# Operand buffers of the matrix products placed at a fixed distance modulo 256 bytes

## The chip, the core and the metric

The kernel runs on one core of a Trainium2 chip, as one program in one launch. The metric is the time of one execution in device microseconds (us); smaller is better. In the kernel before, the median of three runs is 2753.42 us (2751.35 to 2754.86).

A core has a tensor engine (PE in the profile) that multiplies a stationary operand (up to 128 x 128, loaded first, "PEld") with a moving operand (128 rows and up to 512 columns that stream through), both from the on-chip memory SBUF, into the accumulators PSUM; a vector engine (DVE), a scalar engine (ACT), a general one (POOL), and queues that start DMA transfers (SP above all). SBUF has 128 partitions; an address here is a byte offset inside a partition, the same for all 128.

## The reference

256 tokens of width 1024, batch 1, float32. A first block of two layers and a second of four layers follow one another:

```
for layer in range(2):
    x = x + 0.5 * swiglu(rmsnorm(x), ffn1_w_in, ffn1_w_out)      # 1024 -> 2 x 2816 -> 1024
    h = rmsnorm(x)
    x = x + (attn_lru_mixer(h) if layer == 0 else deltanet_mixer(h))
    x = x + cross_attention(rmsnorm(x), rmsnorm(mem))            # mem: 256 x 1024
    x = x + 0.5 * swiglu(rmsnorm(x), ffn2_w_in, ffn2_w_out)
x = rmsnorm(x)
for i, mixer in enumerate((retention, conformer_conv, gla, retention)):
    x = x + rmsnorm(mixer(rmsnorm(x)))
    x = x + rmsnorm(relu(rmsnorm(x) @ w_up) ** 2 @ w_down)       # 1024 -> 4096 -> 1024
```

Nearly all of the arithmetic is in products of the 256 tokens with float32 weight matrices.

## The kernel before, in words

**Values in two parts.** Activations are kept transposed, channels on partitions, tokens along the free dimension, so a chunk of 128 channels is a tile of 128 x 256. For accuracy each operand of a product with weights is split into a high part and a rest, both of type float32r, and three products are made: high weights with both parts of the activations, the weights' rest with the high part (`mm3`, line 204; `mm_split`, line 252, does the same for attention values). All go through `mm` (line 201), so in the profile nearly all products have line 202.

**Weights.** The weight matrices come from memory as one long stream of pieces, each of 8 blocks of 128 x 128 (512 KB), in the order of use. `fetch` (line 158) loads a piece into one of three `raw` buffers (SP queue). `block` (line 166) splits it: ACT copies it to `whi` (line 179), DVE subtracts to get `wlo` (line 180); five buffers of each (pool `wp`). A block serves three products of 256 columns, so a piece serves 24.

**Products.** `gemm` (line 211) has the weight block stationary and the activations moving, 256 columns; either the inputs are the outer loop (all outputs' high-part products first, then those with the activations' rest) or it takes one output after the other with `mm3`. `gemm_rows` (line 236) makes outputs with tokens on partitions: there the activations are stationary and four weight blocks move, 512 columns. Outputs take turns in four PSUM banks (pool `ps`).

**Moving operands by name.** `xs`: the normalised input of a layer, split (pool `xsp`, four buffers, `prep` at line 353). `h`: the hidden values of the feed-forward parts (`ffn`, line 528, and `mlp`, line 1703), input of their second matrix. `os`: what a mixer or an attention hands to its output matrix. `memS`: the memory's normalised values in cross-attention (`xa`, line 555). `kq`: the delta-net's output (`dn`, line 792). `pr`, `mem`, `pT`, `pts`: attention weights, multiplied with the values `v`.

**Order and memory.** Engines run their instructions in the order of the program; waits are semaphores that the tile layer sets by data dependence. Each layer opens a pool of its own (`stage`, line 131) and gets tiles from it with `T` (a tag with its number of buffers, line 139) and `one` (line 142); pools that last all along (`cp`, `rawp`, `wp`, `xsp` and others) lie below in SBUF, one after the other in the order of creation. No tile asks for an alignment; a tile starts where the one before ends, and pools are padded.

```
def T(self, tag, shape=(2, S), dt=F32, bufs=2, p=128):
    return self.pool.tile([p, *shape], dt, name=self.nm(tag), tag=tag, bufs=bufs)
```

Of the kernel before, what the change touches and what calls it, by code (L numbers as in the profile page):

```python
# [7 lines left out]
F32 = mybir.dt.float32  # L8
F32R = mybir.dt.float32r
# [8 lines left out]
S = 256  # L18
# [14 lines left out]
CONV_STEP = (3, 6)  # L33

# [27 lines left out]
class Lazy:  # L62
    """A norm's factors, emitted in two steps: the sums, then (when first asked for) the values."""
# [16 lines left out]
class Kernel:  # L80
    def __init__(self, ctx, tc, A):
        self.ctx, self.tc, self.nc, self.A = ctx, tc, tc.nc, A
        nc = self.nc

        def pool(name, bufs, **kw):
            return ctx.enter_context(tc.tile_pool(name=name, bufs=bufs, **kw))

        self.cp = pool("cp", 1)
        self.rawp = pool("rawp", 3)
        self.wp = pool("wp", 5)  # L90
        self.xsp = pool("xsp", 4)
        self.tp = pool("tp", 2)
        self.sp = pool("sp", 4)
        self.psp = pool("ps", 4, space=bass.MemoryType.PSUM)
        self.pmp = pool("pm", 4, space=bass.MemoryType.PSUM)
        self.order = []
        self.piece = -1
        self.at = NB
        self.x, self.ready, self.next_gain, self.hold = [], [], None, {}
        self.n, self.raws = 0, []  # L100
        self.par = self.cp.tile([128, N_PAR], F32, name="par")
        nc.scalar.dma_start(self.par[:, 0:16], A["par"][:, 0:16])
        for p in range(4):
            t = self.cp.tile([128, 2, S], F32, name=f"x{p}")
            nc.sync.dma_start(t, A["x"][:, 2 * p:2 * p + 2, :])
            self.x.append(t)
            if p < 2:
                self.fetch(p, 2 - p)
        nc.scalar.dma_start(self.par[:, 16:], A["par"][:, 16:])
        self.ident = self.cp.tile([128, 128], F32, name="ident")  # L110
        nc.scalar.dma_start(self.ident, A["ident"])
        self.ones = self.cp.tile([128, 128], F32, name="ones")
        nc.gpsimd.memset(self.ones, 1.0)
        self.inv = self.cp.tile([128, 2], F32, name="inv")
        nc.gpsimd.memset(self.inv[:, 0:1], 1.0 / D)
        nc.gpsimd.memset(self.inv[:, 1:2], 1.0 / 512)
        self.onesw = self.cp.tile([128, S], F32, name="onesw")
        nc.gpsimd.memset(self.onesw, 1.0)
        self.both = self.cp.tile([128, 8], F32, name="both")
        nc.vector.tensor_tensor(self.both, self.P("final_norm", 0, 8), self.P("norm_gains_2", 0, 8), op=OP.mult)  # L120
# [9 lines left out]
    @contextmanager  # L130
    def stage(self):
        """The memory of one part of the computation."""
        with ExitStack() as es:
            old = getattr(self, "pool", None)
            self.pool = es.enter_context(self.tc.tile_pool(name=self.nm("st"), bufs=1))
            yield
            self.pool = old

    def T(self, tag, shape=(2, S), dt=F32, bufs=2, p=128):
        return self.pool.tile([p, *shape], dt, name=self.nm(tag), tag=tag, bufs=bufs)  # L140
# [17 lines left out]
    def fetch(self, piece, n=1):  # L158
        """Loads a piece of the weights, in n transfers."""
        raw = self.rawp.tile([128, NB * 128], F32, name=self.nm("raw"), tag="raw")  # L160
        w = NB * 128 // n
        for i in range(n):
            self.nc.sync.dma_start(raw[:, i * w:i * w + w], self.A["w"][piece][:, i * w:i * w + w])
        self.raws.append(raw)
# [26 lines left out]
    def hold_back(self, ahead, act, dve):  # L191
        """The split of the pieces so many ahead comes after these instructions."""
        for n in ahead:
            self.hold.setdefault(self.piece + n, []).append((act, dve))

    def behind(self, ins, other):
        """Queues ins behind other on their engine."""
        if other is not None:
            self.tc.add_manual_dep(ins.ins, other.ins.name, mybir.DependencyInfo(mybir.DependencyClass.NoSync, mybir.DependencyReason.DATA), reason="behind")
# [11 lines left out]
    def gemm(self, name, groups, src, k_outer, calls={}):  # L211
        """groups: psum pairs with the m of each half; k_outer walks the inputs in the outer loop.
        calls: what to emit after step n (an input or, without k_outer, an output)."""
# [22 lines left out]
    def gemm_rows(self, name, m0, src, calls={}):  # L236
        """Outputs [token, 512 columns]: two banks, one for each 128 tokens."""
        outs = [self.psum((512,)) for _ in range(2)]
        nk = len(src)
        for k in range(nk):  # L240
            wh, wl = self.block(name, k, m0, 4)
            xh, xl = src[k]
            for t, o in enumerate(outs):
                s = slice(t * 128, t * 128 + 128)
                self.mm(o, xh[:, s], wh, k == 0, False)
                self.mm(o, xh[:, s], wl, False, False)
                self.mm(o, xl[:, s], wh, False, k == nk - 1)
            if k in calls:
                calls[k]()
        return outs  # L250

    def mm_split(self, out, a, b, first, last):
        """out (+)= a.T @ b, both given as (hi, lo)."""
# [4 lines left out]
    def split_rows(self, v, outs, y):  # L258
        """v [128, 2 (hi, lo), 2, 512] from two psum tiles scaled by token."""
# [4 lines left out]
    def split(self, t, src_ap, scale=1.0):  # L264
        """t [128, 2 (hi, lo), 2, 256] from a pair."""
# [8 lines left out]
    def rsqrt(self, ms, w, tag="rs"):  # L274
        """1/sqrt of a [128, w] tile."""
# [16 lines left out]
    def quick_rsqrt(self, ms):  # L292
        """-2/sqrt of each column of a [128, 2] psum, the columns in turn."""
# [20 lines left out]
    def token_sums(self, tiles, one=None):  # L314
        """Sums over partitions of [128, 256] tiles: a [128, 2] psum with tokens on partitions."""
# [9 lines left out]
    def rows(self, cols, pb=None):  # L325
        """Per-token values [128, 2] as a psum [128, 256] with the value of token t in column t."""
# [5 lines left out]
    def add_square(self, acc, sq, p, eps=EPS):  # L332
        """Adds pair p of squares up; after the last one, both halves too."""
# [10 lines left out]
    def stats(self, acc, one=None):  # L344
        """-2/sqrt of the sums over partitions of acc times one; one's inverse times EPS / 128 is in acc."""
# [7 lines left out]
    def prep(self, src, x, gain, tiles=None):  # L353
        """Appends the split parts of pair x times its gains to src."""
        nc = self.nc
        t = self.xsp.tile([128, 2, 2, S], F32R, name=self.nm("xs"), tag="xs") if tiles is None else tiles()
# [7 lines left out]
    def updated(self, p):  # L364
        """Pair p of x is final in this part: its split for the next part."""
# [3 lines left out]
    def norm(self, x, gain, tiles=None, rbt=None):  # L369
        """x: four pairs. Returns the split inputs times the gain, and (to be called) each token's factor as columns and as rows."""  # L370
# [19 lines left out]
    def two_norms(self):  # L390
        """As norm, for rmsnorm(rmsnorm(x) * final_norm): the factors of both norms together, and the first one's rows."""
# [48 lines left out]
    def residual(self, name, src, scale, first=1):  # L440
        """x += scale * (src @ w); the first pairs of outputs walk the inputs together."""
# [16 lines left out]
    def post_norm(self, name, src, gain, bias=None):  # L458
        """x += rmsnorm(src @ w [+ bias]) * gain."""
# [61 lines left out]
    def keep_clock(self, t, n):  # L521
        """Products nobody reads, for the time in which the tensor engine would wait and lose its clock."""
# [32 lines left out]
    def xa(self, l):  # L555
        nc = self.nc
        with self.stage():
# [62 lines left out]
            for n in range(2):  # L620
                outs = self.gemm_rows(("xa_wkv", l), 8 + 4 * n, msrc, {1: rest[0], 3: rest[1], 7: rest[2]} if n == 0 else {})
                v = self.T("v", (2, 2, 512), F32R, 1)
# [11 lines left out]
    def gate_half(self, name, c, w):  # L634
        """Half of a parameter, as a small tile."""
# [4 lines left out]
    def log1p_exp(self, z, w):  # L640
        """log(1 + exp(-|z|)) of a [128, w] tile, by the series of atanh."""
# [25 lines left out]
    def softplus_neg(self, z, w):  # L667
        """softplus(-z) = max(-z, 0) + log(1 + exp(-|z|))."""
# [123 lines left out]
    def dn(self):  # L792
        nc = self.nc
        W = ("dn_w_in", 0)
        with self.stage():
# [18 lines left out]
            wab = self.one((8, 16))  # L814
# [14 lines left out]
            def parts(m, after):  # L829
                """The product's quarters; after the last one, what becomes of it."""  # L830
# [12 lines left out]
            def conv_silu(m, out, g):  # L843
                """out [128, 2, 256]: twice the silu of the convolution."""
# [13 lines left out]
            def gates():  # L858
                """beta / 4, log of beta's inverse, the sums of the log decays."""
# [56 lines left out]
            def decays(b):  # L916
                """Exponents of four heads: rows and, per source, columns."""
# [94 lines left out]
            def level_2(lev, p):  # L1012
                """The even columns of the inverse and the odd ones of its transpose."""
# [103 lines left out]
            def weave(main, side):  # L1117
                """Emits both lists, the second spread over the first."""
# [89 lines left out]
    def rotary_tables(self):  # L1208
        """cos and sin of position * frequency, frequencies on partitions: reduced by multiples of 2 pi in three parts."""
# [31 lines left out]
    def ret(self, i, final=False):  # L1241
# [3 lines left out]
        with self.stage():  # L1245
# [72 lines left out]
            for h in range(4):  # L1318
# [14 lines left out]
                vs[h] = self.T("v", (2, 2, 512), F32R, 1)  # L1333
# [22 lines left out]
    def conv(self, i):  # L1356
# [3 lines left out]
        with self.stage():  # L1360
# [75 lines left out]
            def about_six():  # L1436
                """Sums over six chunks of the distance to their mean and of its square."""
# [94 lines left out]
    def gla(self, i):  # L1532
        nc = self.nc
        W = ("gla_w_in_2", 0)
        with self.stage():
            w1 = self.one((8, 64))
# [7 lines left out]
            wmr = self.one((128,))  # L1544
# [65 lines left out]
            def values(n, calls={}):  # L1610
                outs = self.gemm_rows(W, 8 + 4 * n, src, calls)
                v = self.one((2, 2, 512), F32R)
# [3 lines left out]
            def scores(h):  # L1616
                q, k = qk[0][:, h], qk[1][:, h]
                ptile = self.T("ptl")
                for d in range(2):
# [9 lines left out]
                    # (source tile, queries, columns of the query tile)  # L1629
# [99 lines left out]
def stages(k):  # L1729
    """Each part of the computation with the gains of its first norm."""  # L1730
# [30 lines left out]
def chunks(v):  # L1761
    """[..., 128 c] to [128, ... c] with the vector's place in the first axis."""
# [90 lines left out]
```

## Time and profile before

| | |
|---|---|
| median of three runs | 2753.42 us (2751.35 to 2754.86) |
| span of the profiled execution (first to last instruction) | 2748.4 us |
| mean granted clock of the tensor engine | 0.994 |
| PE busy | 2708.3 us, 99% of the span, 21804 products |
| DVE busy | 1892.7 us, 69% |
| ACT busy | 1419.8 us, 52% |
| POOL busy | 81.6 us, 3% |
| DMA | 449.17 MB, mean 163 GB/s |

The profile gives the profiled execution's time as this span alone; the runs' median lies 5.0 us above it. A row of the costliest groups reads: line, engine, operation, output tile <- input tiles, shapes, count | busy us, mean ns of one. For a product the first input named is the moving operand. A product's duration counts from its start to its modelled end; products overlap, so their durations sum to more than the time. A row of a timeline reads: start us, us from the first start to the last end, engine, line, operation, and how many equal instructions in a row it merges. A row of the windows reads: stretch in us, its length, then busy us and (x count) of PE, PEld, DVE, ACT and POOL, then the granted clock, the DMA engines' busy share and GB/s. A wait reads: who <- for whom: us in total, times, longest us.

### The profile page before, as it was taken

What the parts mean: (1) busy time and instruction counts of PE and PEld (TensorE: products, weight loads), DVE (VectorE), ACT (ScalarE), POOL (GpSimd) and SP (SyncE); (2) the same over time, 40 slices, a digit from 0 to 9 for tenths busy, and PEclk for the clock granted to TensorE, in tenths of its full rate; (3) what the DMA queues carried; (4) which work ended last, traced back from release to release, by engine and by line L of the source; (5) the groups of instructions that cost most, each with busy time, mean ns of one, the idle gap of its engine ahead of it and who ended that gap; (6) DMA issues with size and microseconds to landing.
All of it is one profiled execution on the core that took longest, in us unless ns stands there. A gap on an engine that the chain in (4) does not pass through costs nothing.

```text
span 2748.4 us, 52619 instructions
## 1 busy us (share of the span) xinstructions
PE 2708.3 (99%) x21804; PEld 2639.8 (96%) x21804; DVE 1892.7 (69%) x3043; ACT 1419.8 (52%) x2005; POOL 81.6 (3%) x102
## 2 busy tenths in 40 slices
PE   8999999999999999999999999989999999999998
PEld 8998999999999999999999999989999999899998
DVE  7757867657678676766876756877468764876754
ACT  5446554444457655545455544346447654545553
POOL 0000000000010000000000001800000000000000
PEclk9999999999999999999999999989999999999999
DMA  6554545555543144555544654225544555445553
GB/s 221 184 194 134 189 153 178 185 182 185 184 157 127 63 154 158 183 184 177 165 159 155 199 187 150 85 74 195 185 153 142 160 184 189 155 146 185 169 184 123
DMA packets 125343, 449.17 MB, mean 163 GB/s; under 512 B 14192, under 2 KB 15216, under 8 KB 125104
## 3 DMA queue, kind: packets, MB, share of 16 engines
q1 hardware_dynamic: 121680, 440.46, 49.4%
q10 hardware_dynamic: 3424, 5.37, 0.6%
q8 instruction: 170, 2.79, 0.4%
q14 instruction: 69, 0.57, 0.1%
HBM read 444.72 MB, written 1.05 MB: 162 GB/s over the span
## 4 chain that ended last, share of the span: by engine, by line
PE 93%; DVE 3%; ACT 1%; DMA 1%; POOL 1%; issue 1%; SPq 0%; POOLq 0%; DVEq 0%; ACTq 0%
PE ps L202 84%; PE pm L202 9%; DVE wlo L180 1%; DMA raw<-w 1%; POOL pacc L1398 0%; ACT whi L179 0%; POOL dg L1475 0%; DVE pt L512 0%; DVE x L513 0%; DVE xs L360 0%; DVE pt L506 0%; DMA one<-gla_w 0%; PE pm L767 0%; PE pm L581 0%; ACT XX L1025 0%
## 5 line engine op out<-in xcount | busy, mean ns | idle before, releaser
L180 DVE TENSOR_TENSOR wlo<-raw,whi 128x1024 fp32r<-128x1024 f32 (+1 forms) x837 | 1025.6, 1228 | 553.1 <-ACT whi L179 551.8
L179 ACT ACTIVATE whi<-raw 128x1024 fp32r<-128x1024 f32 (+1 forms) x837 | 884.0, 1058 | 987.8 <-PE ps L202 778.6
L202 PE MATMUL ps<-xs,whi 128*128 128x256 f32 x7424 | 1360.8, 285 | 7.3 <-ACT whi L179 6.8
L202 PEld LDWEIGHTS ps<-xs,whi 128*128 128x128 f32 x7424 | 1163.8, 192 | 11.5 <-ACT whi L179 6.8
L202 PE MATMUL ps<-xs,wlo 128*128 128x256 f32 x3712 | 1039.9, 284 | 0.3 <-DVE wlo L180 0.3
L202 PEld LDWEIGHTS ps<-xs,wlo 128*128 128x128 f32 x3712 | 713.8, 192 | 2.2 <-issue 1.3
L202 PE MATMUL ps<-h,whi 128*128 128x256 f32 x3456 | 610.9, 279 | 0.0
L202 PEld LDWEIGHTS ps<-h,whi 128*128 128x128 f32 x3456 | 527.7, 187 | 0.0
L202 PE MATMUL ps<-h,wlo 128*128 128x256 f32 x1728 | 473.0, 279 | 0.0
L202 PEld LDWEIGHTS ps<-h,wlo 128*128 128x128 f32 x1728 | 324.6, 188 | 0.0
L202 PE MATMUL ps<-os,whi 128*128 128x256 f32 x1152 | 205.5, 281 | 3.4 <-ACT os L267 3.4
L202 PEld LDWEIGHTS ps<-os,whi 128*128 128x128 f32 x1152 | 177.8, 190 | 4.2 <-ACT os L267 3.7
L202 PE MATMUL ps<-os,wlo 128*128 128x256 f32 x576 | 156.1, 281 | 0.0
L202 PE MATMUL ps<-whi,xs 128*128 128x512 f32 x352 | 113.9, 397 | 0.0
L437 DVE TENSOR_TENSOR t<-ps,rbc 128x512 f32<-128x512 f32 x116 | 79.6, 690 | 48.2 <-PE ps L202 45.6
L202 PEld LDWEIGHTS ps<-os,wlo 128*128 128x128 f32 x576 | 109.6, 190 | 0.0
L202 PEld LDWEIGHTS ps<-whi,xs 128*128 128x128 f32 x352 | 65.9, 188 | 13.2
L267 ACT ACTIVATE h<-t 128x512 fp32r<-128x512 f32 x108 | 67.9, 629 | 18.1 <-DVE t L550 16.5
L269 DVE TENSOR_TENSOR h<-t,h 128x512 fp32r<-128x512 f32 x108 | 74.3, 688 | 0.8 <-ACT h L267 0.5
L359 ACT ACTIVATE xs<-x,par 128x256 fp32r<-128x256 f32 x120 | 53.9, 499 | 32.2 <-DVE x L508 20.9
L202 PE MATMUL ps<-wlo,xs 128*128 128x512 f32 x176 | 69.1, 393 | 0.7 <-DVE wlo L180 0.6
L1717 DVE SCALAR_TENSOR_TENSOR t<-ps,rbc 128x512 f32<-128x512 f32 x64 | 43.8, 690 | 30.3 <-PE ps L202 29.7
(425 smaller groups left out, 2425.0 us busy)
## 6 DMA issues: line engine op xcount, KB each, us to landing
raw<-w SPq DMA_DIRECT2D x835, 512.0 KB, 3.6
mem<-mem ACTq DMA_DIRECT2D x8, 256.0 KB, 5.2
x<-x SPq DMA_DIRECT2D x4, 256.0 KB, 5.8
os<-ret_dist ACTq DMA_DIRECT2D x2, 512.0 KB, 3.8
out<-x SPq DMA_DIRECT2D x4, 256.0 KB, 2.3
raw<-w SPq DMA_DIRECT2D x2, 256.0 KB, 4.8
one<-lru_w ACTq DMA_DIRECT2D x1, 512.0 KB, 4.6
par<-par ACTq DMA_DIRECT2D x1, 333.5 KB, 4.9
```

The lines of the kernel that those rows point to most:

```text
L179: a = nc.scalar.activation(hi[:, i:i + w], raw[:, i:i + w], AF.Copy)
L180: b = nc.vector.tensor_tensor(lo[:, i:i + w], raw[:, i:i + w], hi[:, i:i + w].bitcast(F32), op=OP.subtract)
L202: self.nc.tensor.matmul(out, lhsT, rhs, start=start, stop=stop, skip_group_check=True)
L267: nc.scalar.activation(t[:, 0], src_ap, AF.Copy, scale=scale)
L269: nc.vector.tensor_tensor(t[:, 1], src_ap, t[:, 0].bitcast(F32), op=OP.subtract)
L359: nc.scalar.activation(t[:, 0, i], x[:, i], AF.Copy, scale=g)
L437: self.nc.vector.tensor_tensor(t, ps, self.bc(rb), op=OP.mult)
L1717: nc.vector.scalar_tensor_tensor(a, g[0], 0.0, self.bc(rb), op0=OP.max, op1=OP.mult)
```

## The change

Buffers move; the computation stays. A filler of 48 float32 (`cpad`, 192 bytes) is put into the pool `cp`, so that all that lies behind it starts 192 bytes later, the weight buffers among them. The tiles of the moving operands named in `MOVING`, and `xs`, are aligned to 256 bytes. The tiles of attention values are made 64 bytes longer and used from byte 64 on (`values_tile`). Three small tiles of the delta-net and the gated layer are put into buffers of other tags (`c2`, `ptl`), which takes no room of their own. The docstrings and one comment are dropped.

```diff
+MOVING = ("h", "os", "memS", "kq", "pr", "pts", "mem", "pT")
...
         nc.gpsimd.memset(self.inv[:, 1:2], 1.0 / 512)
+        self.cp.tile([128, 48], F32, name="cpad")
         self.onesw = self.cp.tile([128, S], F32, name="onesw")
...
     def T(self, tag, shape=(2, S), dt=F32, bufs=2, p=128):
-        return self.pool.tile([p, *shape], dt, name=self.nm(tag), tag=tag, bufs=bufs)
+        return self.pool.tile([p, *shape], dt, name=self.nm(tag), tag=tag, bufs=bufs, align_bytes=256 if tag in MOVING else None)
+
+    def values_tile(self, tag, bufs=1):
+
+        n = self.nm("v")
+        t = self.pool.tile([128, 2064], F32R, name=n, tag=tag or n, bufs=bufs, align_bytes=256)
+        return t[:, 16:].rearrange("p (a b c) -> p a b c", a=2, b=2)
...
-        t = self.xsp.tile([128, 2, 2, S], F32R, name=self.nm("xs"), tag="xs") if tiles is None else tiles()
+        t = self.xsp.tile([128, 2, 2, S], F32R, name=self.nm("xs"), tag="xs", align_bytes=256) if tiles is None else tiles()
...
-                v = self.T("v", (2, 2, 512), F32R, 1)
+                v = self.values_tile("v")
...
-            wab = self.one((8, 16))
+            wab = self.T("c2", (8, 16))
...
-                vs[h] = self.T("v", (2, 2, 512), F32R, 1)
+                vs[h] = self.values_tile("v")
...
-            w1 = self.one((8, 64))
+            w1 = self.T("ptl", (8, 64))
...
-            wmr = self.one((128,))
+            wmr = self.T("ptl", (128,))
...
-                v = self.one((2, 2, 512), F32R)
+                v = self.values_tile(None)
```

The two built programs have the same instructions in the same order on every engine, and the same waits but for one: ACT waits for DVE once more ahead of a `c2` tile of the delta-net layer. What differs is addresses. The profile shows no addresses; the table has them from the two programs. The distance is the start of the moving operand less that of the stationary one, in bytes, modulo 512 (modulo 256 in brackets). Within a kind it is the same for every product, since blocks and halves of tiles lie multiples of 512 bytes apart.

| moving, stationary (products of float32r) | columns | products | distance before | distance after |
|---|---|---|---|---|
| xs, weights | 256 | 11136 | 0 (0) | 192 (192) |
| h, weights | 256 | 5184 | 320 (64) | 192 (192) |
| os, weights: two retention layers, gated layer | 256 | 768 + 192 | 320 (64) | 192 (192) |
| os, weights: two cross-attention layers | 256 | 384 | 320 (64) | 448 (192) |
| os, weights: first mixer | 256 | 192 | 448 (192) | 192 (192) |
| os, weights: convolution layer | 256 | 192 | 0 (0) | 448 (192) |
| memS, weights | 256 | 384 | 320 (64) | 448 (192) |
| kq, weights | 256 | 192 | 320 (64) | 192 (192) |
| pr, mem, pT, pts, values | 256 | 336 | 0 (0) | 192 or 448 (192) |
| weights, xs | 512 | 528 | 0 (0) | 320 (64) |
| weights, memS | 512 | 192 | 192 (192) | 64 (64) |

The first weight buffer `whi` starts at byte 41856 before and 42048 after, the first `xs` at 82816 and 83200.

## Rows read from the trace of the kernel before

**Rows 1.** The page: span, busy us of each engine, chain by engine.

```profile
span 2748.4 us, 52619 instructions
...
PE 2708.3 (99%) x21804; PEld 2639.8 (96%) x21804; DVE 1892.7 (69%) x3043; ACT 1419.8 (52%) x2005; POOL 81.6 (3%) x102
...
PE 93%; DVE 3%; ACT 1%; DMA 1%; POOL 1%; issue 1%; SPq 0%; POOLq 0%; DVEq 0%; ACTq 0%
```

**Rows 2.** Waits of PE, of ACT and of the SP queue, the longest each.

```profile
PE ps L202 <- ACT whi L179: 6.8, 1, 6.8
...
ACT whi L179 <- PE ps L202: 778.6, 520, 6.2
...
SPq L163 <- DVE wlo L180: 2164.4, 767, 41.7
```

**Rows 3.** The page, costliest groups: products of xs and of h with weights.

```profile
L202 PE MATMUL ps<-xs,whi 128*128 128x256 f32 x7424 | 1360.8, 285 | 7.3 <-ACT whi L179 6.8
...
L202 PE MATMUL ps<-xs,wlo 128*128 128x256 f32 x3712 | 1039.9, 284 | 0.3 <-DVE wlo L180 0.3
...
L202 PE MATMUL ps<-h,whi 128*128 128x256 f32 x3456 | 610.9, 279 | 0.0
...
L202 PE MATMUL ps<-h,wlo 128*128 128x256 f32 x1728 | 473.0, 279 | 0.0
```

**Rows 4.** Windows: xs; h; os of first mixer, cross-attention, retention, convolution.

```profile
60.00:120.00 60.00, 60.00 (x502) 60.00 (x502) 41.68 (x46) 27.65 (x31) 0.00 (x0) 1.00 0.57 185
140.00:180.00 40.00, 40.00 (x342) 40.00 (x342) 21.23 (x22) 17.71 (x21) 0.00 (x0) 1.00 0.56 185
281.00:300.00 19.00, 19.00 (x170) 19.00 (x169) 16.59 (x24) 12.46 (x18) 0.00 (x0) 1.00 0.58 185
388.00:405.00 17.00, 17.00 (x153) 17.00 (x152) 12.49 (x17) 11.07 (x16) 0.00 (x0) 1.00 0.49 157
1460.00:1490.00 30.00, 30.00 (x257) 30.00 (x256) 15.04 (x14) 14.46 (x20) 0.00 (x0) 1.00 0.59 188
1824.00:1832.00 8.00, 8.00 (x69) 8.00 (x68) 6.39 (x9) 4.48 (x9) 0.00 (x0) 1.00 0.81 248
```

**Rows 5.** Timeline of PE: delta-net gates, stationary operand of 16 columns.

```profile
803.32 2.89 PE L202 MATMUL pm<-xs,one 128*16 128x256 f32 x24
```

**Rows 6.** Timeline of PE: first products of os in the first mixer.

```profile
278.72 0.39 PE L202 MATMUL ps<-os,whi 128*128 128x256 f32 x1
278.94 0.28 PE L202 MATMUL ps<-os,wlo 128*128 128x256 f32 x1
279.06 0.28 PE L202 MATMUL ps<-os,whi 128*128 128x256 f32 x1
279.18 0.28 PE L202 MATMUL ps<-os,wlo 128*128 128x256 f32 x1
279.30 0.28 PE L202 MATMUL ps<-os,whi 128*128 128x256 f32 x1
279.41 0.28 PE L202 MATMUL ps<-os,wlo 128*128 128x256 f32 x1
```

**Rows 7.** The chain of waits in order of time: its number of pieces.

```profile
909 pieces in order of time: start us, us, what
```

**Rows 8.** Timeline of PE: 512 columns, stationary xs, then memS.

```profile
1390.11 0.62 PE L202 MATMUL ps<-whi,xs 128*128 128x512 f32 x2
1390.56 0.39 PE L202 MATMUL ps<-wlo,xs 128*128 128x512 f32 x1
1390.79 0.62 PE L202 MATMUL ps<-whi,xs 128*128 128x512 f32 x2
...
373.31 0.63 PE L202 MATMUL ps<-whi,memS 128*128 128x512 f32 x2
373.77 0.39 PE L202 MATMUL ps<-wlo,memS 128*128 128x512 f32 x1
374.01 0.63 PE L202 MATMUL ps<-whi,memS 128*128 128x512 f32 x2
```

**Rows 9.** Window around the depthwise convolution.

```profile
1680.00:1800.00 120.00, 111.57 (x860) 108.89 (x858) 98.89 (x203) 51.21 (x99) 69.00 (x70) 0.96 0.28 86
```

## The prediction

> **What bounds the kernel now.** I read the page from the top: the span, the busy line, the chain that ended last. TensorE (PE) is busy 99% of the span, VectorE (DVE) 69%, ScalarE (ACT) 52%, and PE alone makes 93% of the chain [rows 1]. Then the waits: the longest that PE has is 6.8 us, once, at the start, while ACT's split of the weights waits 778.6 us for PE to give buffers back and the DMA queue waits 2164.4 us for the splits to do so [rows 2]. Everything that feeds PE runs ahead of it. So the time is the number of products times the time from one product's start to the next one's, the interval; a gain there is a gain of the kernel nearly everywhere.
>
> The mean duration of a product (285 and 284 ns for xs, 279 for h [rows 3]) is not that interval, since products overlap; but the two differ in the same direction. The interval comes from windows in which PE does one kind of product: a window counts every product that runs in it, so also the 2.4 (283 / 120) that began before it. I set it beside the distance of the two operands from the table in the section on the change:
> - xs, distance 0: 60.00 us / (502 - 2.4) = 120.1 ns
> - h, distance 64: 40.00 / (342 - 2.4) = 117.8 ns
> - os of the retention layer, distance 64: 30.00 / (257 - 2.4) = 117.8 ns
> - os of the convolution layer, distance 0: 8.00 / (69 - 2.4) = 120.1 ns
> - os of the cross-attention layer, distance 64: 17.00 / (153 - 2.4) = 112.9 ns
> - os of the first mixer, distance 192: 19.00 / (170 - 2.4) = 113.4 ns
>
> All of that is [rows 4]. [...] Lower than 113 I find nothing: 24 products with only 16 stationary columns take 2.89 us, the last one's 0.28 included [rows 5], so (2.89 - 0.28) / 23 = 113.5 ns with hardly any weight load. I take 113.3 ns as the floor of 256 columns.
>
> **What the change does, part by part.** No instruction is added, taken away or moved on PE, DVE, POOL or SP; only addresses differ. After it, all 256-column products with weights, and those with attention values, stand at distance 192. I take 113.3 ns for them, the value of the one stretch seen at that distance (192 products, two orders, four PSUM banks).
> - xs: 7424 + 3712 = 11136 products [rows 3] x (120.0 - 113.3) = 74.2 us
> - h: 3456 + 1728 = 5184 [rows 3] x (117.8 - 113.3) = 23.0 us
> - os of both retention layers and the gated one: 768 + 192 = 960 x 4.4 = 4.3 us
> - os of the convolution: 192 x 6.7 = 1.3 us; os of the first mixer and of both cross-attention layers, 576, are at the floor already: 0
> - memS, kq and the attention values: 384 + 192 + 336 = 912, in short runs between other work; 0 to 6.7 ns each, 0 to 6 us; I take 3, since the nearest long runs (h) give 4.4 ns each
>
> Together 105.8 us. Against it:
> - Restarts. The stretch at distance 192 did not begin at 113: its first four intervals sum to 0.47 us (278.94 to 279.41 [rows 6]) and at the floor would take 0.453, so 17 ns are lost each time PE comes from other work. The chain has 909 pieces [rows 7], at most every second one a run of these products: 0 to 455 x 17 ns = 7.7 us. Restarts before aren't at their steady value either, so I take 4.
> - Products of 512 columns, where weights are the moving operand. The change puts them at distance 64, which the trace doesn't show for this width. Distance 0 (xs) gives 1390.79 - 1390.11 = 0.68 us for three, 226.7 ns, twice the floor; distance 192 (memS) gives 374.01 - 373.31 = 0.70, 233.3 [rows 8]. 528 are at 226.7 now and 192 at 233.3. Ends: all at 226.7, 192 x 6.6 = 1.3 us gained; all at 233.3, 528 x 6.6 = 3.5 us lost. I take a loss of 1, the middle.
> - Where PE waits for others, a product that ends sooner only waits longer. From 1680 to 1800 us, around the depthwise convolution, PE is busy 111.57 of 120 us [rows 9]; the gain of the 384 products of that layer's first weight matrix (2.6 us) may go there whole. With the delta-net layer I take 3 us; ends 0 and 6.
> - The three loads that now land in buffers of c2 and ptl, and one more wait on ACT ahead of a c2 tile: I cost them at nothing. The readers of those loads are done in the opening of their layers, and ACT, 52% busy, is ahead of PE; if that cover were gone it would be one ACT operation, about 1 us, once.
>
> 105.8 - 4 - 1 - 3 = 98 us. The profiled span is 2748.4, so about 2650; the median of the runs, 2753.4, lies 5.0 us above the span, which I leave as it is: 2753.4 - 98 = 2655, stated as 2656.
>
> [...] Rows 4 show one line's interval go with the place of its operands. [...]
>
> **The rivals.**
> 1. *Distance 192 has a second, slower gait.* Distance 64 has two: 117.8 in h and retention, 113 in cross-attention [rows 4], with the same weight buffers. What sets off which I can't read from the trace; the history just ahead of a run is my guess. For it: one stretch at 192 is little. Against it: that stretch came down to 113 by itself within five products [rows 6]. If all ran at 117.8: xs gains 11136 x 2.2 = 24.5 us, conv os 0.4, 576 os lose 2.6: 2731. A mixture by layers lies between 2668 and 2731. 14 in 100.
> 2. *The pattern repeats every 512 bytes, not 256 (slower).* The stretch seen stands at 448 modulo 512; after the change xs, h and most of os stand at 192 modulo 512, which no row shows. Distances 0, 320 and 448 modulo 512 gave 120.1, 117.8 or 113, and 113.4; the unseen one could be worse than 0 by the same step again, 6.7 ns: 126.7. Place: xs, h, os. Price: 11136 x 6.7 + (5184 + 960) x 8.9 = 74 + 55 = 129 us, so 2882. It decides as soon as xs stands above 120. Against it: 113.3 to 120.0 and 226.7 to 233.3 are equal steps of 6.67 ns, about the time of 16 columns (113.3 x 16 / 256 = 7.1), 64 bytes, which speaks for a short period. 6 in 100.
> 3. *Place has nothing to do with it:* layer, data or history set the interval, and nothing changes: 2753. Against it: os at 120.1 in one layer and 113.4 in another, xs at 120 in all. 5 in 100.
> 4. *Another engine becomes the bound.* A block of weights serves 24 products, so it would last 24 x 113.3 = 2.72 us instead of 2.88. In xs stretches DVE is busy 41.68 of 60 us and ACT 27.65 [rows 4]; in 56.7 us that is 74% and 49%, and the DMA queue has its waits to spend [rows 2]. If half of the gain were lost so: 2705. 3 in 100.
>
> **How the numbers follow.** The forecast has the remaining 72 in 100, its own span 2645 (nothing lost, the sum's upper ends) to 2668 (all losses at their ends). To reach 8 in 10 the range takes in half of rival 1 and rival 4: 2645 to 2705. Runs of before lie within 3.5 us of each other; 0.2%, 5.5 us, is about what a measurement can tell from no change. Faster by more: 72 + 14 + 3 = 89; within it: 5; slower: 6.
>
> **What would show it.** In the new profile: xs products in the first feed-forward layer at 113.3 ns (some 530 in a 60 us window instead of 502), h the same; mean durations near 276 ns instead of 283 and 279; the 512-column ones between 226.7 and 233.3; os of the first mixer and of cross-attention as before; PE's share of the chain still above 90%. Wrong is the forecast if h or xs stand at 117 or 118 in some layers (rival 1), above 120 (rival 2), or if PE's waits for DVE or DMA grow by tens of us (rival 4).

## The result, and the profile after

The changed kernel takes 2718.4 us (median of four runs, 2713.0 to 2720.1) against 2752.4 us of the kernel before on the same chips: a ratio of 0.9876, 95% interval 0.9862 to 0.9890. It is faster by 34 us, where 98 were forecast; 2718 lies outside the range of 2645 to 2705.

Page of the kernel after: span and instructions, busy time by engine, chain by engine, costliest groups. These are the lines that answer to [rows 1] and [rows 3]; lines of the kernel have moved by 8, so 202 is now 210.

```profile
span 2710.9 us, 52620 instructions
...
PE 2665.3 (98%) x21804; PEld 2594.5 (96%) x21804; DVE 1889.4 (70%) x3043; ACT 1421.1 (52%) x2005; POOL 82.2 (3%) x102
...
PE 92%; DVE 4%; ACT 2%; DMA 1%; issue 1%; POOL 0%; SPq 0%; ACTq 0%; DVEq 0%; POOLq 0%
...
L210 PE MATMUL ps<-xs,whi 128*128 128x256 f32 x7424 | 1324.6, 282 | 7.4 <-ACT whi L187 6.7
...
L210 PE MATMUL ps<-xs,wlo 128*128 128x256 f32 x3712 | 1026.4, 281 | 1.0 <-DVE wlo L188 0.9
...
L210 PE MATMUL ps<-h,whi 128*128 128x256 f32 x3456 | 610.9, 281 | 0.0
...
L210 PE MATMUL ps<-h,wlo 128*128 128x256 f32 x1728 | 475.8, 281 | 0.0
```

PE is still what the kernel waits for: busy 98%, 92% of the chain, its longest wait 6.7 us, once, at the start. The group of h and `whi` reads 610.9 us, the very number of [rows 3]: h gained nothing. xs gained less than half of what was forecast (31.5 of 74.2 us by the summed intervals below).

Windows of the kernel after, answering to [rows 4] (from:to, sum, PE busy and products, granted clock, share of the DMA engines, GB/s). The first two are xs and h of the first feed-forward layer, the third xs of another layer; then os of the first mixer, xs and os of the first retention layer, and os of the convolution layer:

```profile
60.00:120.00 60.00, 60.00 (x511) 1.00 0.57 191
140.00:180.00 40.00, 40.00 (x342) 1.00 0.58 187
450.00:510.00 60.00, 60.00 (x512) 1.00 0.58 185
...
281.00:300.00 19.00, 19.00 (x170) 1.00 0.59 197
1405.00:1425.00 20.00, 20.00 (x179) 1.00 0.67 207
1440.00:1465.00 25.00, 25.00 (x223) 1.00 0.63 202
1794.00:1804.00 10.00, 10.00 (x87) 1.00 0.63 191
```

Read as before, with 2.4 products taken off for those that began earlier: 60 / (511 - 2.4) = 118.0 and 40 / (342 - 2.4) = 117.8 ns in the feed-forward layer, 113.4 in the first mixer, 20 / (179 - 2.4) = 113.3 and 113.3 in retention, 118.2 in the convolution layer. All of these stand at the same distance, 192. So **distance 192 has two gaits** (two steady intervals), 113.3 and 117.8 ns.

To see how they are spread, I took the start-to-start intervals of every PE row in the trace. Of 18,672 products that come in unbroken runs of nine or more, 13,102 went at 117.8 and 5,250 at 113.3; the rest are the depthwise convolution, whose places the change does not set. Once a run has taken a gait it keeps it to the end, over changes of weights, of PSUM bank and from xs to h. The eight longest runs, one in each feed-forward layer (1,390 to 1,558 products from just behind the spreading of the per-token factors to the end of the layer), all took 117.8; the 650 products of each retention layer's gates and output took 113.3. By kind, the summed intervals went from 1363.0 to 1331.5 us for xs, stayed at 610.6 for h, and went from 208.3 to 204.5 for os.

### The profile page after: what moved, and what is told of

It is laid out like the page before. It is cut to its first block, busy times and chain, and to the rows that moved or that the text cites. A ratio compares the mean times of both kernels' runs of the same rounds, so it can differ in the third digit from the quotient of the medians.

```text
span 2710.9 us, 52620 instructions
## 1 busy us (share of the span) xinstructions
PE 2665.3 (98%) x21804; PEld 2594.5 (96%) x21804; DVE 1889.4 (70%) x3043; ACT 1421.1 (52%) x2005; POOL 82.2 (3%) x102
## 4 chain that ended last, share of the span: by engine, by line
PE 92%; DVE 4%; ACT 2%; DMA 1%; issue 1%; POOL 0%; SPq 0%; ACTq 0%; DVEq 0%; POOLq 0%
PE ps L210 83%; PE pm L210 9%; DVE wlo L188 1%; DMA raw<-w 1%; ACT whi L187 1%; POOL dg L1483 0%; DMA mem<-mem 0%; DVE pm L1395 0%; DVE pt L520 0%; DMA os<-ret_dist 0%; DVE x L521 0%; DVE xs L368 0%; DVE pt L514 0%; DMA ptl<-gla_w 0%; ACT XX L1033 0%
## 5 line engine op out<-in xcount | busy, mean ns | idle before, releaser
L210 PE MATMUL ps<-xs,whi 128*128 128x256 f32 x7424 | 1324.6, 282 | 7.4 <-ACT whi L187 6.7
L210 PEld LDWEIGHTS ps<-xs,whi 128*128 128x128 f32 x7424 | 1144.6, 190 | 11.6 <-ACT whi L187 6.7
L210 PE MATMUL ps<-xs,wlo 128*128 128x256 f32 x3712 | 1026.4, 281 | 1.0 <-DVE wlo L188 0.9
L210 PEld LDWEIGHTS ps<-xs,wlo 128*128 128x128 f32 x3712 | 699.8, 189 | 3.0 <-DVE wlo L188 1.6
L210 PE MATMUL ps<-h,whi 128*128 128x256 f32 x3456 | 610.9, 281 | 0.0
```

The source lines that it names most:

```text
L210: self.nc.tensor.matmul(out, lhsT, rhs, start=start, stop=stop, skip_group_check=True)
```

## Experiments

Three theories stood at the start. **A:** the place of the operands decides which gaits there are, and something just ahead of a run picks one of them. **B:** place does nothing, and the gait belongs to layer and history. **C:** place decides which gaits there are, but the product ahead does not pick one: the gait belongs to the stretch of the program, or is drawn anew at each start.

**Sixteen distances in two kernels.** The weights stand at 128 modulo 256, and xs and h are shifted inside 256-byte-aligned tiles by a number that depends on the feed-forward layer:

```diff
-        self.cp.tile([128, 48], F32, name="cpad")
+    def shifted(self, pool, tag, off, bufs=None):
+        t = pool.tile([128, 1084], F32R, name=self.nm(tag), tag=tag, bufs=bufs, align_bytes=256)
+        return t[:, off:off + 1024].rearrange("p (a b c) -> p a b c", a=2, b=2)
...
+        k.off = OFFS.get(n, 0)
```

> Weights at 128 modulo 256; xs and h of the eight feed-forward layers at distances 0, 32, 64, 96 (the four of the first block), 128, 160, 192, 224 (the four of the second) modulo 256; all other xs, os and memS at 128. Theory A (place sets which gaits exist, the start of a run which of them it takes): distance 0 at 120.0 ns, 64 and 192 at 117.8 or 113.3, the six others at one of these or a new value, steady within each layer; near 117.8 on the average, some 2720 us. Theory B (place has no effect, the layer sets the gait): the eight layers stand at 117.8 whatever their distance, as they do after the change. A distance that shows 113.3 in a whole layer would be a candidate for a better version.

> As the scan in steps of 32, with distances 240, 208, 176, 144 in the feed-forward layers of the first block and 112, 80, 48, 16 in those of the second. Theory A: values between those of the neighbours 32 bytes apart, from 113.3 to 120.0 ns, some distances without the gait of 117.8. Theory B: 117.8 in all eight layers.

The two ran once each, 2748.8 and 2734.8 us, with 2750.5 for the kernel before. Windows of 40 us in the h products of a layer: of the first kernel at distances 0, 32, 64 and 192, then of the second at 144, 112, 80 and 16:

```profile
148.00:188.00 40.00, 40.00 (x336) 1.00 0.56 182
544.00:584.00 40.00, 40.00 (x346) 1.00 0.57 194
731.00:771.00 40.00, 40.00 (x342) 1.00 0.56 190
...
2255.00:2295.00 40.00, 40.00 (x342) 1.00 0.57 190
```

```profile
1232.00:1272.00 40.00, 40.00 (x346) 1.00 0.58 193
1592.00:1632.00 40.00, 40.00 (x355) 1.00 0.62 195
1927.00:1967.00 40.00, 40.00 (x336) 1.00 0.55 183
...
2639.00:2679.00 40.00, 40.00 (x339) 1.00 0.57 187
```

The clock column is 1.00 in all of them. The mean start-to-start intervals of the h products, from the rows themselves (40 / (count - 2.4) gives the same within 0.4):

| distance | 0 | 16 | 32 | 48 | 64 | 80 | 96 | 112 |
|---|---|---|---|---|---|---|---|---|
| ns | 120.0 | 118.7 | 116.7 | 118.3 | 117.8 | 120.0 | 120.0 | **113.3** |

| distance | 128 | 144 | 160 | 176 | 192 | 208 | 224 | 240 |
|---|---|---|---|---|---|---|---|---|
| ns | 118.7 | 116.7 | 120.0 | 119.2 | 117.8 | 119.2 | 118.3 | 117.1 |

xs in the same layers agrees within 0.5 ns. The same eight layers, which all had 117.8 in the kernel after, now have another interval with each place: theory B falls. Each entry is what one layer took at that place, after one start; whether the place has a second gait, the scans do not show. Distance 192, put at other addresses than in the kernel after (weights at 128, xs at 64), again gives 117.8. And 112, where no product of either kernel stood, is at the floor for a whole layer.

**Steps of four bytes** about 112 and 192, the same edit with other numbers:

```diff
-OFFS = dict(zip((...), (32, 40, 48, 56, 0, 8, 16, 24)))
+OFFS = dict(zip((...), (58, 59, 61, 62, 14, 15, 17, 18)))
```

> Distances by feed-forward layer, in steps of 4 bytes about the two places that showed 113.3 ns: 104, 108, 116, 120 in the four feed-forward layers (ffn1_0, ffn2_0, ffn1_1, ffn2_1) and 184, 188, 196, 200 in mlp_0 to mlp_3; xs products of the mixers at 128. Theory P1 (gaits depend on the place in broad steps): 104 to 120 within 1 ns of 113.3, and 184 to 200 at 113.3 or 117.8. Theory P2 (112 and 192 are narrow places): the neighbours at 116 to 120 ns. No bound on the total: 2735 to 2750 us under P2, 2700 to 2730 under P1.

One run, 2771.9 us. Windows in the h products at 116 and at 188:

```profile
741.00:781.00 40.00, 40.00 (x331) 1.00 0.56 180
...
1953.00:1993.00 40.00, 40.00 (x338) 1.00 0.57 185
```

By intervals: 104 and 108 give 120.0, 116 gives 121.7, 120 gives 122.0; 184, 196 and 200 give 120.0, 188 gives 119.2. Four bytes off, 112 loses 6.7 to 8.3 ns. Theory P2 of the expectation holds: these are narrow places, not valleys. The total came out 22 us above P2's upper end; against the kernel before, h alone took 12.7 us more by summed intervals (623.3 for 610.6), since it stood at 119 to 122 in all eight layers, where the kernel before had 117.8, and os, memS and the 512-column products took 5.5 more.

**What picks the gait.** The kernel after, with 92 products added in the feed-forward layers that nobody reads, of 16 to 256 moving columns:

```diff
+    def nudge(self, t, stage, m):
+        n = 16 * ((3 * m + 2 * stage) % 16 + 1)
+        self.mm(self.psm((S,))[:, 0:n], t[:, 0:128], t[:, 0:n])
...
```

> The changed kernel with 92 products that nobody reads, spread over the eight feed-forward layers ahead of an output pair, each with 16 to 256 moving columns in steps of 16: they break the long runs of equal products. Theory A (two gaits, the start decides): after some of them the run goes on at 113.3 ns instead of 117.8, after others at 117.8, by their width; if half of the products end at the faster gait, 11900 x 0.5 x 4.45 = 26 us less, with 92 x 0.12 = 11 us for the products themselves: some 2703. Theory C (the slower gait is forced by what else runs in these layers: splits by ACT and DVE, or DMA): all stretches stay at 117.8 and the time is 2718 + 11 = 2729.

One run: 2701.5 us, 17 us less than the kernel after although 92 products were added. PE's timeline of this kernel (start, duration, line, operation), the rows of three added products in the first layer:

```profile
66.23 0.28 PE L210 MATMUL pm<-xs 128*128 128x256 f32 x1
...
77.66 0.19 PE L210 MATMUL pm<-xs 128*128 128x48 f32 x1
...
88.67 0.21 PE L210 MATMUL pm<-xs 128*128 128x96 f32 x1
```

and windows of nine microseconds ahead of, between and behind them:

```profile
56.00:65.00 9.00, 9.00 (x82) 1.00 0.61 190
67.00:76.00 9.00, 9.00 (x78) 1.00 0.55 184
78.50:87.50 9.00, 9.00 (x82) 1.00 0.57 187
89.50:98.50 9.00, 9.00 (x82) 1.00 0.60 199
```

82 products in a window are 9 / (82 - 2.4) = 113.1 ns each, 78 are 119.0 (117.8 by the rows' own intervals): the product of 256 columns turns the fast gait to the slow one, 48 turns it back, 96 leaves it fast. Of the 88 added products that the trace shows, 84 fall into a running gait, and for each width and each gait met there was one outcome only:

| columns added | met 117.8, then | met 113.3, then |
|---|---|---|
| 16 | 113.3 (4 times) | 117.8 (1) |
| 32, 48, 208 | 113.3 (16) | not seen |
| 64, 80 | 113.3 (2) | 113.3 (7) |
| 96 | not seen | 113.3 (5) |
| 112, 144 | 113.3 (2) | 117.8 (10) |
| 128, 240, 256 | not seen | 117.8 (15) |
| 160 | 117.8 (5) | 117.8 (1) |
| 176 | 113.3 (4) | 117.8 (1) |
| 192 | 113.3 (5) | 113.3 (1) |
| 224 | 113.3 (1) | 117.8 (4) |

So the gait is a state that one added product moves, of xs by xs and 16 to 256 columns here; the widths that met the same gait more than once did the same each time. For a run under way theory C falls: one layer holds both gaits, and nothing in these outcomes looks drawn. Whether the start of a run behind other work is drawn is another matter, which the next experiment comes back to.

**The gain bought back with eight products.** The kernel after with one unread product of 80 columns, and for contrast of 240, in each feed-forward layer (the comments in this and later edits are added here):

```diff
+                if j == 4:                  # feed-forward; in the mlp layers j == MLP_FIRST + 1
+                    self.reset(src[0][0])   # self.mm(psm[:, 0:RESET], t[:, 0:128], t[:, 0:RESET])
```

> The kernel after with 8 unread products added, one in each feed-forward layer, some 70 to 94 products behind the layer's restart: a float32r product of 80 moving columns, xs by xs. In the run with many unread products 4 of 4 such products of 80 columns left a 113.3 ns run at 113.3, and the one that met a 117.8 ns run turned it to 113.3. Theory A (place offers the gaits, and the product ahead of a run picks one, which then lasts to the end of the run): the 8 long runs hold 11,732 products at 117.8 ns in the kernel after; all but some 620 of them go to 113.3: 11,100 x 4.45 ns = 49 us, less 8 x 0.13 us for the added products: 2718.4 - 48 = 2670 us (2664 to 2680), with 113.3 ns in all eight layers, xs and h alike. Rival C (the gait is not set by a product's width; each interruption draws it anew): some layers at 113.3 and some at 117.8, 2690 to 2705 us. Rival D (long runs fall back to 117.8 by themselves): 2710 us or more.

> The same 8 unread products at the same places, 240 moving columns in place of 80. In the run with many unread products 5 of 5 such products turned a 113.3 ns run to 117.8. Theory A: the eight long runs stay at 117.8 ns, the time is that of the kernel after plus 8 x 0.13 us, about 2719.5 us (2715 to 2723). Rival C (any interruption draws the gait anew): about half of the layers at 113.3, 2685 to 2705 us.

With 80 columns: 2669.3 us (four runs, 2668.7 to 2672.2), a ratio of 0.9706 to the kernel before (0.9692 to 0.9721): 49 us less than the kernel after for eight products more, as expected within a microsecond. The page and PE's timeline of the kernel with 80 columns, about the product added in the first layer:

```profile
L211 PE MATMUL ps<-xs,whi 128*128 128x256 f32 x7424 | 1298.7, 279 | 7.6 <-ACT whi L188 7.1
...
L211 PE MATMUL ps<-h,whi 128*128 128x256 f32 x3456 | 587.9, 276 | 0.0
```

```profile
32.93 0.40 PE L211 MATMUL ps<-xs,whi 128*128 128x256 f32 x2
...
33.28 0.20 PE L211 MATMUL pm<-xs 128*128 128x80 f32 x1
33.32 0.48 PE L211 MATMUL ps<-xs,whi 128*128 128x256 f32 x2
```

From 32.93 to 33.28 three products take 0.35 us; behind the added one h is at 113.3 ns to the end of the layer, and the h group falls from 610.9 to 587.9 us, 23 us, the number in the forecast's sum for h. All eight layers do so.

With 240 columns the kernel took 2693.0 us (one run), where 2719.5 was expected. Windows of xs in the first feed-forward layer and in an mlp layer:

```profile
60.00:120.00 60.00, 60.00 (x532) 1.00 0.60 196
1520.00:1560.00 40.00, 40.00 (x342) 1.00 0.59 187
```

113.3 ns in the four feed-forward layers, 117.8 in the four mlp layers. My expectation had read the earlier runs wrongly: 240 had been seen to turn 113.3 into 117.8, never what it does to a run at 117.8, which it met in the feed-forward layers and turned to 113.3, four times of four. In the mlp layers it stood right behind the spreading of the factors. The total lies in the range that was written for a gait drawn anew, but four and four by the kind of layer does not look like a draw.

Starts of runs behind other work are less settled. In the first mixer the two kernels, with 80 and with 240 columns, make the same products at the same addresses, some 1,600 of them, from the added one on (read from the two programs), and both run at 113.3 up to eight products of 128 columns. PE's timeline of these eight and a window behind them, with 80 columns and then with 240:

```profile
224.09 0.93 PE L211 MATMUL pm<-qk 64*128 64x128 f32 x8
...
225.90:232.40 6.50, 6.50 (x60) 1.00 0.32 110
```

```profile
224.44 0.93 PE L211 MATMUL pm<-qk 64*128 64x128 f32 x8 [0.21 <-ACT one L732]
...
226.20:232.70 6.50, 6.50 (x57) 1.00 0.31 108
```

The first goes on at 113.3, the second at 117.8 (by the rows' own intervals). The one difference that these rows show is a wait of 0.21 us for ACT. In the same way gates and output of the last retention layer ran at 113.3 in the kernel after and at 117.8 in both kernels with eight products. So the product just ahead does not settle every start; whether a wait's length does, or chance, no run tells apart.

**Distance 112 throughout.** No added products; xs and h at 112 in every layer, os and memS at 128, kq at 32. The edit is against the kernels of the scans:

```diff
-        k.off = OFFS.get(n, 0)
+        k.off = OFFS.get(n, 60)      # and 60 for every name in OFFS: 240 less 128
```

> No added products: all xs and h tiles at 112 modulo 256 ahead of the weights (weights at 128, xs and h 240 modulo 256), os, memS and kq products at 128 or 32. Theory A1 (112 has the floor gait alone): xs and h at 113.3 ns in all 16,320 products, against 120.0 and 117.8 before: 74 + 23 us, less about 2 us for os and memS at 118.8: some 2660 us (2653 to 2668). Theory A2 (112 has several gaits too, and the one layer at 112 in the earlier scan began on the floor by luck): some long runs at 115 to 120 ns, 2680 to 2735 us.

2673.3 us (2669.7 to 2677.3), ratio 0.9721 (0.9702 to 0.9741). Windows of xs and h in the first feed-forward layer, and of os, at 128 here, in the first mixer:

```profile
60.00:120.00 60.00, 60.00 (x532) 1.00 0.61 195
140.00:180.00 40.00, 40.00 (x356) 1.00 0.60 198
...
281.00:300.00 19.00, 19.00 (x165) 1.00 0.69 214
```

xs and h at 113.3 in all eight layers, without help. The start of the first of these long runs, PE's timeline of the same kernel:

```profile
25.13 0.28 PE L214 MATMUL ps<-xs,wlo 128*128 128x256 f32 x1
...
25.48 0.28 PE L214 MATMUL ps<-xs,wlo 128*128 128x256 f32 x1
```

From 25.13 to 25.48 three products take 0.35 us, as slow as at 192; but ten products on, the run is at 113.3. So are all 37 runs of forty or more products at this distance, behind whatever work: most within ten products, all within 20. So A1 holds for the gait: at 112 the floor comes back by itself. Distance 128, though, showed two values in this kernel, in the os windows of a retention layer and of the gated layer:

```profile
1420.00:1450.00 30.00, 30.00 (x255) 1.00 0.57 184
...
2074.00:2086.00 12.00, 12.00 (x102) 1.00 0.54 173
```

By the rows' own intervals they are 118.7 and 120.0 ns, so more places than 192 have a second gait. The missing 13 us of the expectation are partly seen: os took 210.3 us by summed intervals, 2.0 more than in the kernel before, memS 0.9 more, and the 512-column products, now at 144 or 128, 3.4 more (172.5 for 169.1).

**112 for os and memS too:**

```diff
+        if tag in ("os", "memS"):
+            t = self.pool.tile([128, 1088], dt, name=self.nm(tag), tag=tag, bufs=bufs, align_bytes=256)[:, 60:1084]
...
```

To make room, two os tiles of a retention layer share a buffer, and the attention values of the gated layer go back to distance 0.

> The kernel at distance 112 with os and memS tiles at 112 modulo 256 as well (kq at 32; two of the small kinds of tile give up their alignment for the space). In the run with xs and h at 112 every one of the some 20 runs of such products came to 113.3 ns within 14 products, whatever stood ahead of it, while os at 128 took 118.9 and memS 119.0. Theory A1: 1,728 os products x (118.9 - 113.4) = 9.5 us and 384 memS products x 5.6 = 2.1 us go: 2673.3 - 11.6 = 2662 us (2657 to 2668). Rival (os differs by where it is written or by its neighbours in memory): os stays at 117 to 120 ns and the time at 2670 to 2677.

2668.7 us (five runs, 2666.6 to 2669.8), ratio 0.9706 (0.9693 to 0.9719): the fastest version here, level with the eight added products. The os window of the first mixer, which answers to the last one above:

```profile
281.00:300.00 19.00, 19.00 (x170) 1.00 0.71 238
```

19 / (170 - 2.4) = 113.4 ns in place of 116.9. os fell from 210.3 to 203.8 us and memS from 46.8 to 44.9, 8.4 of the 11.6 expected; products outside the kinds named took 3 us more in this profile, for which I have no cause.

**An added product at every restart.** The kernel after, with 80 columns ahead of the first product of every part and behind every spreading of factors, the latter of `wlo` by `wlo`:

```diff
+        self.reset(self.cur[1])      # at the end of rows(): 80 columns of wlo by wlo
...
         if k_outer:
+            self.reset(src[0][0])
```

> The kernel after with an unread product of 80 columns in every place where a restart has been seen: behind each set of products that spreads per-token values, and ahead of the first product of every part (72 in all, 64 more than in the kernel with eight). The kernel with eight left 2,468 products at 117.8 ns: 11 us. Theory A: most of them go to 113.3: 11 us, less 64 x 0.12 = 8 us of added products (fewer where the engine waits anyway, ahead of a part): 2666 us (2660 to 2674). If the gait of the short runs is not picked by the product ahead of them: 2675 us or more.

2697.0 us (2693.9 to 2697.4): 28 us worse than with eight, and far outside the expected 2660 to 2674. By summed intervals xs took 28.2 us more (1332.1 for 1303.9): its long runs went at 117.8 in all eight feed-forward layers. PE's timeline of this kernel at an mlp layer's start, and of the kernel with eight at the same place:

```profile
1489.48 0.60 PE L210 MATMUL pm<-ident,qo 128*128 128x128 f32 x4
1489.85 0.28 PE L210 MATMUL pm<-wlo 128*128 128x80 f32 x1
```

```profile
1469.67 0.60 PE L211 MATMUL pm<-ident,qo 128*128 128x128 f32 x4
1470.03 0.28 PE L211 MATMUL pm<-xs 128*128 128x80 f32 x1
```

The same steps at the same spacing, and ahead of them both kernels ran at 113.3. Behind `wlo` by `wlo` the xs of all four mlp layers ran at 117.8, behind xs by xs at 113.3. So columns alone do not pick the gait; the operands of the product ahead matter too. Whether it is their place was not tried.

**The kernel before, with the gait of h nudged.** xs stays at distance 0, h at 64:

```diff
+            self.reset(hs[0][0])     # 80 columns of h by h, ahead of the first h product
             self.residual((f"{which}_w_out", l), hs, 0.25)
...
```

> The kernel before (xs at distance 0, h at 64) with one unread product of 80 columns (h by h) ahead of the first h product of each of the eight feed-forward layers. Theory A: distance 64 offers both gaits (the cross-attention os products there ran at 113.3), so h goes from 117.8 to 113.3 in most layers without any move of a buffer, 5,184 x 4.45 = 23 us, less 1 us: 2750 - 22 = 2728 us; xs stays at 120.0 in every stage. Rival (113.3 belongs to distances 192 and 112 and h at 64 has 117.8 alone): 2751 us, h at 117.8 in all eight.

2747.5 us (one run; the kernel before 2749.5). Windows of this kernel, xs and then h of the first layer:

```profile
60.00:120.00 60.00, 60.00 (x502) 1.00 0.57 185
160.00:200.00 40.00, 40.00 (x342) 1.00 0.58 185
```

xs at 120.1, h at 117.8, in all eight layers. The rival of this expectation came about. It fits that h at 64 has the one gait only, but an added product that happens to pick the slow one would look the same; os at 64 did run at 113 in cross-attention [rows 4]. This stays open.

## Why the prediction was wrong

- **What bounds the kernel: right.** PE did before and does after. With xs and h at 112 the xs window holds 532 products in 60 us, PE's longest wait is 7.2 us, at the start, its longest for DVE 2.8 us, and DVE is busy 71%: neither DVE nor the loads took the gain. Rival 4 had no part in it.
- **"I take 113.3 ns for them, the value of the one stretch seen at that distance": this step failed.** The stretch was 192 products that follow other work than the feed-forward layers' do. Behind the spreading of the factors, where nearly all xs and h products begin, all eight long runs took 117.8. In the kernel after 13,102 products pay 117.78 - 113.33 = 4.45 ns: 58 us of the 62 between the stated 2656 and 2718. The kernel with eight added products shows it the other way round: move the gait of those runs, at unchanged places, and 49 us come back.
- **Rival 1 was the case**, priced 2668 to 2731 and given 14 in 100. My reason against it, that the stretch came down to 113 by itself within five products, was wrong: in the kernel after no run at 192 that had taken 117.8 came down by itself, one of 1,558 products included. Distance 64 with its two values in [rows 4] should have carried more weight, since it showed that place alone did not fix the interval.
- **xs, 74.2 us.** 120.0 to 117.8 is a third of the step; with part of the mixers' xs at the floor 31.5 us were gained. With everything at the floor (distance 112 for xs, h, os and memS) it was 62.4: intervals within runs fell by 66.6 us, from a mean of 119.9 to 113.9 since short runs spend part of their length settling, and 4 us were lost at breaks. So for distance 112 the term was also too large by about 12 us, which the 4 us for all restarts did not cover. For 192 no run had all of xs at the floor; an estimate from the kernel with eight products is 59.1 us gained (1363.0 to 1303.9), and 7.5 more for some 1,690 products of xs left at 117.8: about 67, 7 below the term.
- **h, 23.0 us.** 0 in the kernel after: h takes over the gait that xs had, and 117.8 at 192 is 117.8 at 64. Its size was right: 23 us when the gait is fast.
- **os, 5.6 us:** 3.8; the convolution layer's os took the slow gait (118.2 ns in its window). **The small groups, 3 us:** memS gave 0.5 and the attention values about 1.
- **Products of 512 columns, -1 us:** -0.7 by summed intervals. PE's timeline of the kernel after, which answers to [rows 8], at distance 64 for both kinds:

```profile
1373.79 0.62 PE L210 MATMUL ps<-whi,xs 128*128 128x512 f32 x2
...
1374.48 0.62 PE L210 MATMUL ps<-whi,xs 128*128 128x512 f32 x2
...
368.66 0.62 PE L210 MATMUL ps<-whi,memS 128*128 128x512 f32 x2
...
369.35 0.39 PE L210 MATMUL ps<-whi,memS 128*128 128x512 f32 x1
```

  0.69 us for three is 230 ns in both: midway between the ends that were set.
- **Rival 2, a period of 512 bytes,** fell: no xs run of the kernel after stands above 118.4 ns, and at 112 and 192 alike the layers reach 113.3 wherever their tiles lie modulo 512. **Rival 3,** by which place does nothing, fell as well: the scans show 113.3 to 122.0 ns at a clock of 1.00, in the same layers with other places. Why place matters, they do not show.
- The few microseconds put down to waits were not measured apart. The added wait of ACT and the three loads in shared buffers do not show among the long waits of the kernel after: PE's second longest is 3.4 us, for os, as before.

## What to carry to other kernels

Where TensorE is the bound and the interval differs between stretches of one shape, scan the place of the operands in small steps, some layers each, before fixing it: here it was worth 3%, and a good place lay four bytes from a bad one. Prefer a place at which every long run comes to the floor by itself (112 here, 2668.7 us) to one that reaches it only from some starts (192, 2718.4 us). And when a trace shows a value in one stretch alone, price the work by what precedes it: the short stretch behind other work, 192 products at 113.4 ns, was no sample for the long ones, which took 117.8 here.

## What the runs showed of the hardware

- The interval between float32r products of 256 columns, each with its own weight load of 128 columns (PEld x21804 for 21804 products), went from 113.3 to 122.0 ns with the distance of their two operands modulo 256 bytes, at a granted clock of 1.00. That it is the distance, and not the moving operand's place alone, rests on one comparison: xs at 0 modulo 256 ran at 118.7 with the weights at 128 (in the scan) and at 113.3 or 117.8 with the weights at 64 (the kernel after). In all scans and in the kernels at 112 the weights stood at 128.
- At one and the same distance PE can hold either of two intervals (113.33 or 117.78 at 192) for more than 1,300 products, and one added product (0.19 us at 48 columns, 0.28 at 256) moves it from one to the other, repeatably by its length and the gait it meets. Width is not all that counts: 80 columns of `wlo` and 80 of xs, at the same spot, picked different gaits, and behind the same eight products of 128 columns one kernel took 113.3 and another 117.8.
- What in PE or in the buffers makes 112 differ from 108 and 116, and what state the gait is, none of these runs shows.
